# The weights of every second column block of an MLP matrix are split by two transfers and a ScalarE negation

## The chip, the cores and the metric

One NeuronCore of a Trainium2 chip runs the kernel. The metric is the device time of one launch in microseconds (us). A core has TensorE (PE, matrix products; PEld is its loading of weights), VectorE (DVE), ScalarE (ACT), GpSimd (POOL), and SyncE (SP), which issues transfers. Data moves from device memory (HBM) into the on-chip memory SBUF over 16 DMA engines; TensorE writes its sums into PSUM.

## The reference

A hybrid transformer block on 256 latent tokens and 256 context tokens, width 2048, depth 1. The part that the change touches is the MLP at its end:

```python
def sq_relu_mlp(h, w_in, w_out):
    return jnp.square(jax.nn.relu(h @ w_in)) @ w_out

h2 = modulate(rmsnorm(x, norm2_g[i]), sh2, sc2)
x = x + gt2 * sq_relu_mlp(h2, w_mlp_in[i], w_mlp_out[i])
return rmsnorm(x, final_norm_g)
```

`w_mlp_in` is 2048 x 8192, `w_mlp_out` 8192 x 2048. Before it stand a bidirectional gated linear attention, a Fourier branch, their gates and an output projection, and a modulation by products of a vector with a 2048 x 12288 matrix.

## The kernel before

**Precision by splitting.** The inputs are float32. TensorE is fed with a rounded 4-byte type (fp32r). To keep the precision, each operand is held as a high and a low part: `split` lets ScalarE write `hi`, the value rounded to fp32r, and VectorE `lo = value - hi`. A product is then three matmuls (`mm3`): high by high, high by low, low by high. `wide` does the same with fewer instructions: the two parts of the activations lie side by side, 512 columns, and are multiplied with the high part of the weight in one matmul; the low part of the weight is multiplied with the high part of the activations, 256 columns.

**Units.** All weights after the first input projection are laid out in HBM as a list of blocks of 128 x 2048 floats (1 MiB), the tensor `ws`, in the order in which they are used (`stream`). A unit is one such block: 16 weight tiles of 128 x 128, which give 128 output columns. At the end of the list stands the MLP, in four groups g = 0 to 3 of 2048 hidden columns: 16 units `mi` of the first matrix, then 16 units `mo` of the second. The unit `("mi", j)` holds hidden columns 128 j to 128 j + 127. Between them 16 blocks `mod` of the modulation matrix are strewn over the first 76 units or so; VectorE multiplies these in place and sums them (`mod_unit`), and TensorE does not use them.

**Loading and splitting.** `load_to(i)` issues the loads up to block i. Each gets a tile `raw` out of a pool of six (8 KiB in each partition, 1 MiB in all). SP issues them, in order, and its queue waits until a tile is free. `conv_to(i)` splits the units up to i: for each half (`hf`) of a unit it takes two tiles `w` (4 KiB in each partition) out of a pool of eight, and `split` fills them. So eight `w` tiles hold two units. The raw tile is free when the second subtraction has been done, a `w` tile when its matmuls have been done. `next_gemm` is called when a unit is about to be multiplied: it asks for splitting up to the next unit that is not `mod`, and so for loading up to four blocks beyond that one.

**Multiplying.** In g = 0 a unit `mi` runs `unit_mm` with `mm3`, 48 matmuls of 258 columns (256 tokens and two more for the shift of the modulation); in g = 1 to 3 and for all `mo`, `gemm` and `wide` run 16 matmuls of 512 and 16 of 256 columns. The result, one of eight PSUM banks, is copied by ScalarE, added and squared by VectorE, and split again into the tile `hid`, which the units `mo` of the group read.

**Order.** The order in which the program is written gives priorities; a scheduling pass places the instructions of each engine after a simulated timeline. Except for the first part and the tail, which are pinned, it may move instructions past each other. On the chip each engine and each queue works through its list in order. The semaphores for tiles, their reuse among them, are set by the framework.

GpSimd does nothing before but set four constants. Nearly every instruction goes through a recording helper (`call`, line 147), so that the profile gives L147 for almost all of them; groups are told apart by engine, operation and tile.

Of the kernel before, what the change touches and what calls it, by code (L numbers as in the profile page):

```python
# [8 lines left out]
F32R = mybir.dt.float32r  # L9
U32 = mybir.dt.uint32  # L10
AF = mybir.ActivationFunctionType
ALU = mybir.AluOpType

P = 128
D = 2048
T = 256
KT = D // P
# [59 lines left out]
def name_of(tok):  # L77
    k = tok.rstrip("0123456789")
    return k, int(tok[len(k):] or 0)


def stream():
    seq = []
    order = iter([j * 16 + i for j in (0, 2, 1, 3) for i in range(16)])
    for tok in ORDER:
        k, a = name_of(tok)
        if k == "m":
            seq.append(("mod", next(order)))
        elif k in ("oa", "ob"):
            seq.append(("go", 2 * a + (k == "ob")))  # L90
        elif k in ("q", "gf", "gg", "u", "fg", "wo"):
            seq.append((k, a))
    units = []
    for g in range(4):
        units += [("mi", g * 16 + i) for i in range(16)]
        units += [("mo", (g, m)) for m in range(KT)]
    n = 0
    for i, u in enumerate(units):
        seq.append(u)
        while n < min(16, (i + 1) * 16 // FF_RATE):  # L100
            seq.append(("mod", next(order)))
            n += 1
    return seq
# [3 lines left out]
def tile_block(ctx: ExitStack, tc: tile.TileContext, xT, cT, consts, consts2, consts3, masks, dftc, crow, wlr, wma0, wma, wkv, ws, outT):  # L107
    nc = tc.nc
    cst = ctx.enter_context(tc.tile_pool(name="cst", bufs=1))
    rawp = ctx.enter_context(tc.tile_pool(name="rawp", bufs=6))  # L110
# [7 lines left out]
    def nm(s):  # L118
        cnt[0] += 1
        return f"{s}_{cnt[0]}"  # L120
# [4 lines left out]
    def gr(shape):  # L125
        return gp.tile(shape, F32R, tag="g", name=nm("r"))

    def wr(shape):
        return wp.tile(shape, F32R, tag="w", name=nm("w"))
# [4 lines left out]
    def f(ap):  # L134
        return ap.bitcast(F32)
# [15 lines left out]
    V, S, TE, SY = Pinned(nc.vector), Pinned(nc.scalar), Pinned(nc.tensor), Pinned(nc.sync)  # L151

    def split(hi, lo, src):
        S.copy(hi, src)
        V.tensor_tensor(lo, src, f(hi), op=ALU.subtract)
# [18 lines left out]
    def raw(shape):  # L174
        return rawp.tile(shape, F32, tag="raw", name=nm("raw"))
# [278 lines left out]
    seq = stream()  # L454
    NSQ = len(seq)
    unit_raw = {}
    loaded = [0]

    def load_to(i):
        while loaded[0] <= min(i, NSQ - 1):  # L460
            n = loaded[0]
            unit_raw[n] = raw([P, D])
            SY.dma_start(unit_raw[n], ws[n])
            loaded[0] += 1

    conved = {}
    cpos = [0]

    def conv_to(i):
        while cpos[0] <= min(i, NSQ - 1):  # L470
            n = cpos[0]
            load_to(n + 4)
            if seq[n][0] != "mod":
                his, los = [], []
                for hf in range(2):
                    a, b = wr([P, 8, P]), wr([P, 8, P])
                    split(a, b, unit_raw[n][:, hf * 1024:(hf + 1) * 1024].rearrange("p (k c) -> p k c", c=P))
                    his.append(a)
                    los.append(b)
                conved[n] = (his, los)  # L480
            cpos[0] += 1
# [3 lines left out]
    def next_gemm(kind):  # L485
        while True:
            n = pos[0]
            pos[0] += 1
            k, arg = seq[n]
            if k == "mod" and arg >= 48:  # L490
                mod_unit(n, arg)
                continue
            assert k == kind
            nx = n + 1
            while nx < NSQ and seq[nx][0] == "mod":
                nx += 1
            conv_to(nx)
            return n

    def mod_unit(n, i):  # L500
        load_to(n + 3)
        w = D // MSPLIT
        for j in range(MSPLIT):
            sl = slice(j * w, (j + 1) * w)
            V.scalar_tensor_tensor(unit_raw[n][:, sl], unit_raw[n][:, sl], 1.0, cb[:, sl], op0=ALU.mult, op1=ALU.mult,
                                   accum_out=modp[:, i, j:j + 1])
# [48 lines left out]
    def split_v(s, hf):  # L555
        for blk in range(2):
            a, b = gr([P, 512]), gr([P, 512])
            split(a, b, acc[("v", s, blk, hf)])
            vsp[(s, blk, hf)] = (a, b)

    load_to(4)

    def log_sig(pt, shape):
# [359 lines left out]
    for tok in ORDER:  # L923
        k, a = name_of(tok)
# [13 lines left out]
    for g in range(4):  # L938
        hid = []
        for i in range(16):  # L940
# [15 lines left out]
            a = gr([P, 2, T])  # L956
# [206 lines left out]
```

## Time and profile before

| what | us |
|---|---|
| median of 3 runs | 1458.74 (1458.67 to 1459.31) |
| span of the profiled execution, first to last instruction | 1457.3 |
| TensorE busy | 1434.0 |
| VectorE busy | 1072.1 |
| ScalarE busy | 717.7 |
| 16 DMA engines, mean share of the span by queue 1 | 64.1% |

The profiled execution has no time of its own beside the span; the difference of the span to the median, 1.4 us, is taken for what lies around the instructions. The page of the profile gives busy times per engine, a strip of 40 slices, and the chain of waits: from the last instruction back to whatever released it, step by step. A wait is put down to the event that came last. Matmul ends are modelled, since matmuls overlap, so TensorE's busy time is an upper reading. "SPq" and "DVEq" are the instruction queues of an engine, which issue transfers and semaphore operations.

The MLP takes about the second half of the span: its first unit starts near 726 us, and its last ends near 1444 us.

### The profile page before, as it was taken

The page shows a single profiled execution, that of the slowest core. Times are in us where ns is not written, and L with a number is a line of the kernel's source. Part 1 is how long each engine was busy: PE and PEld are TensorE (multiplying, and loading weights), DVE is VectorE, ACT ScalarE, POOL GpSimd, SP SyncE. Part 2 cuts the span into 40 slices and gives each one's busy share as a digit, 9 for nine tenths or more (in the row PEclk, how much of TensorE's full clock was granted, in tenths as well). Part 3 has the DMA queues.
Part 4 walks back from the last instruction along what each step waited for, and adds up shares of the span by engine and source line. Part 5 has one row for each costly group of instructions (what it writes and reads, how often), then busy time and mean ns, then how long its engine had stood idle before and what let it go on. Part 6 is the DMA issues. An engine that isn't in the chain of part 4 may idle for free.

```text
span 1457.3 us, 22947 instructions
## 1 busy us (share of the span) xinstructions
PE 1434.0 (98%) x9352; PEld 1263.9 (87%) x9352; DVE 1072.1 (74%) x1604; ACT 717.7 (49%) x1091; POOL 0.2 (0%) x4
## 2 busy tenths in 40 slices
PE   6999999999999999999999999999999999999997
PEld 3676789999999999999999988888888888888886
DVE  4666688797989889889876776776766666666666
ACT  6333276665645444455644555444334443344553
POOL 0000000000000000000000000000000000000000
PEclk9999999999999999999999999999999999999998
DMA  9967736355578988888866565666665655554531
GB/s 366 341 260 299 271 141 221 139 195 195 202 264 315 352 330 342 327 325 312 323 242 220 204 257 205 227 235 226 233 228 207 253 180 197 179 197 179 196 123 58
DMA packets 52677, 348.54 MB, mean 239 GB/s; under 512 B 5850, under 2 KB 6106, under 8 KB 13020
## 3 DMA queue, kind: packets, MB, share of 16 engines
q1 hardware_dynamic: 52572, 347.08, 64.1%
q8 instruction: 73, 1.20, 0.3%
q14 instruction: 32, 0.26, 0.1%
HBM read 344.96 MB, written 2.10 MB: 238 GB/s over the span
## 4 chain that ended last, share of the span: by engine, by line
PE 98%; DVE 1%; DMA 0%; ACT 0%; SPq 0%; issue 0%; DVEq 0%
PE ps L147 97%; DVE g L147 1%; PE ps L998 1%; DMA g<-in_xT 0%; SPq L147 0%; ACT g L147 0%; ACT r L147 0%; DVEq L1158 0%; DVE AB L147 0%; DVEq L147 0%
## 5 line engine op out<-in xcount | busy, mean ns | idle before, releaser
L147 PE MATMUL ps<-r,w 128*128 128x512 f32 (+2 forms) x7872 | 1213.1, 315 | 0.0
L147 PEld LDWEIGHTS ps<-r,w 128*128 128x128 f32 x7872 | 1101.4, 188 | 108.4 <-issue 2.0
L147 ACT CAST w<-raw 128x1024 fp32r<-128x1024 f32 (+1 forms) x456 | 470.4, 1036 | 584.5 <-PE ps L147 484.1
L147 DVE TENSOR_TENSOR w<-raw,w 128x1024 fp32r<-128x1024 f32 (+1 forms) x456 | 547.8, 1204 | 255.8 <-ACT w L147 253.1
L147 DVE TENSOR_TENSOR g<-ps,g 128x256 f32<-128x256 f32 (+1 forms) x280 | 140.5, 511 | 56.4 <-PE ps L147 55.0
L147 DVE SCALAR_TENSOR_TENSOR raw<-raw,raw 128x2048 f32<-128x2048 f32 x64 | 146.2, 2284 | 3.3 <-DMA raw<-in_ws 3.3
L147 PE MATMUL ps<-w,r 128*128 128x512 f32 x480 | 118.6, 399 | 1.8 <-ACT r L147 1.8
L147 PEld LDWEIGHTS ps<-w,r 128*128 128x128 f32 x480 | 87.7, 188 | 31.3 <-issue 5.4
L147 DVE TENSOR_TENSOR r<-g,r 128x256 fp32r<-128x256 f32 (+2 forms) x184 | 86.8, 482 | 9.7 <-ACT r L147 8.7
L147 ACT CAST r<-g 128x256 fp32r<-128x256 f32 (+2 forms) x184 | 80.8, 454 | 19.7 <-DVE g L147 13.3
L147 ACT COPY g<-ps 128x256 f32<-128x256 f32 (+3 forms) x153 | 60.2, 402 | 51.3 <-PE ps L147 49.4
L147 ACT ACTIVATE g<-g 128x512 f32<-128x512 f32 (+2 forms) x127 | 64.9, 524 | 23.2 <-DVE g L147 18.2
L147 DVE TENSOR_TENSOR g<-g,g 128x256 f32<-128x256 f32 (+2 forms) x99 | 46.0, 489 | 2.2 <-ACT g L147 1.7
L147 ACT ACTIVATE g<-g,AB 128x256 f32<-128x256 f32 x32 | 17.1, 592 | 45.9 <-DVE AB L147 45.9
L147 PE MATMUL ps<-r,r 128*128 128x256 f32 (+2 forms) x282 | 39.0, 286 | 0.0
L147 PEld LDWEIGHTS ps<-r,r 128*128 128x128 f32 (+1 forms) x282 | 36.3, 188 | 1.3 <-DVE r L147 0.2
L147 DVE SCALAR_TENSOR_TENSOR g<-ps,modc,g 128x256 f32<-128x256 f32 (+1 forms) x56 | 25.1, 453 | 13.4 <-PE ps L147 8.8
L147 PE MATMUL ps<-raw,g 128*32 128x512 f32 (+1 forms) x288 | 34.5, 551 | 0.0
L147 PE MATMUL ps<-g,ones 128*32 128x256 f32 (+1 forms) x78 | 14.0, 534 | 10.9 <-ACT g L147 10.9
L147 PEld LDWEIGHTS ps<-raw,g 128*32 128x32 f32 x288 | 8.4, 109 | 15.3 <-issue 13.1
L147 DVE SCALAR_TENSOR_TENSOR g<-g 128x256 f32<-128x256 f32 x48 | 20.4, 425 | 1.4
L147 PEld LDWEIGHTS ps<-g,ones 128*32 128x32 f32 (+1 forms) x78 | 5.7, 146 | 18.0 <-ACT g L147 17.3
(65 smaller groups left out, 254.8 us busy)
## 6 DMA issues: line engine op xcount, KB each, us to landing
raw<-in_ws SPq DMA_DIRECT2D x276, 1024.0 KB, 4.9
raw<-in_wma SPq DMA_DIRECT2D x32, 1024.0 KB, 8.0
raw<-in_wkv SPq DMA_DIRECT2D x16, 784.0 KB, 8.1
g<-in_xT SPq DMA_DIRECT2D x16, 256.0 KB, 6.7
g<-in_cT SPq DMA_DIRECT2D x8, 256.0 KB, 5.7
out<-g SPq DMA_DIRECT2D x8, 256.0 KB, 2.1
raw<-in_crow SPq DMA_DIRECT2D x1, 1024.0 KB, 5.7
g<-in_dftc SPq DMA_DIRECT2D x3, 256.0 KB, 6.8
```

The source lines that it names most:

```text
L147: r = fn(*a, **k)
L998: tc.keep_in_program_order(nc.tensor.matmul(*a, **k))
```

## The change

Units `mi` with an odd number (32 of 64) are no longer split by `split`. Two tiles of the raw pool, typed fp32r, take their parts. A casting transfer issued by GpSimd fills `a` with the high part straight from HBM. ScalarE writes `-a` into `b`, in two halves. For each half another transfer issued by GpSimd reads the same weights again and adds them to `b`, which then holds weight minus high part, the low part. The matmuls read `a` and `b` in place, so both raw tiles are held until the unit's matmuls have been done, and the unit takes no `w` tiles. `conv_to` has nothing to do for it. Even `mi` units, all `mo` units and the `mod` blocks go on as before; the numbers of units and of matmuls stay.

```diff
+    def by_dma(n):
+        return seq[n][0] == "mi" and seq[n][1] % 2 == 1
+
     loaded = [0]
 
     def load_to(i):
         while loaded[0] <= min(i, NSQ - 1):
             n = loaded[0]
-            unit_raw[n] = raw([P, D])
-            SY.dma_start(unit_raw[n], ws[n])
             loaded[0] += 1
+            if not by_dma(n):
+                unit_raw[n] = raw([P, D])
+                SY.dma_start(unit_raw[n], ws[n])
+                continue
+            a, b = (rawp.tile([P, KT, P], F32R, tag="raw", name=nm("raw")) for _ in range(2))
+            w = ws[n].rearrange("p (k c) -> p k c", c=P)
+            nc.gpsimd.dma_start(a, w)
+            for hf in range(2):
+                sl = slice(8 * hf, 8 * hf + 8)
+                S.mul(b[:, sl, :], f(a)[:, sl, :], -1.0)
+                nc.gpsimd.dma_start(b[:, sl, :], w[:, sl, :], accum_op=ALU.add)
+            unit_raw[n] = ([a[:, 0:8, :], a[:, 8:16, :]], [b[:, 0:8, :], b[:, 8:16, :]])
...
-            if seq[n][0] != "mod":
+            if by_dma(n):
+                conved[n] = unit_raw[n]
+            elif seq[n][0] != "mod":
```

## The prediction

> **What bounds the kernel now.** I read the page first (busy shares, slices, chain of waits), then the chain in order of time, then windows over the MLP, because the change touches nothing else.
>
> ```profile
> PE 1434.0 (98%) x9352; PEld 1263.9 (87%) x9352; DVE 1072.1 (74%) x1604; ACT 717.7 (49%) x1091; POOL 0.2 (0%) x4
> PE   6999999999999999999999999999999999999997
> PEclk9999999999999999999999999999999999999998
> PE 98%; DVE 1%; DMA 0%; ACT 0%; SPq 0%; issue 0%; DVEq 0%
> ```
>
> The chain of waits is TensorE for 98% of the span. Its three long pieces, and what follows them (start, duration, engine, tile, line):
>
> ```profile
> 28.21 314.81 PE ps L147 x2016
> 343.05 1091.67 PE ps L147 x7108
> 1434.72 9.71 PE ps L998 x82
> 1444.45 0.36 DVE g L147
> ```
>
> 314.81 + 1091.67 + 9.71 = 1416.19 us, and from 28.21 to 1444.43 there are 1416.22 us: between its first long run and the tail TensorE never waits for anything that ends up on the path. So an edit that leaves every matmul in place can only win what lies before 28 us or after 1444 us, and this one touches neither. The question is whether it can lose.
>
> The windows show the last projection (640 to 720) and the four phases of the first MLP matrix, one for each column group g = 0 to 3. I placed their borders by the tile shapes: 258-column matmuls mark g = 0, and 16 units of each kind follow one another. Columns: window, length, busy time of PE, PEld, DVE, ACT, POOL with counts, granted clock, share of the 16 DMA engines, GB/s.
>
> ```profile
> 640.00:720.00 80.00, 80.00 (x679) 80.00 (x679) 74.57 (x108) 46.91 (x82) 0.00 (x0) 1.00 0.92 350
> 710.00:720.00 10.00, 10.00 (x87) 10.00 (x86) 8.10 (x19) 6.61 (x20) 0.00 (x0) 1.00 1.00 365
> 726.00:818.00 92.00, 92.00 (x766) 91.91 (x765) 66.20 (x93) 45.92 (x69) 0.00 (x0) 1.00 0.62 228
> 908.00:998.00 90.00, 90.00 (x514) 78.51 (x514) 62.10 (x84) 42.56 (x64) 0.00 (x0) 1.00 0.61 223
> 1088.00:1178.00 90.00, 90.00 (x515) 78.54 (x514) 59.96 (x85) 42.29 (x63) 0.00 (x0) 1.00 0.60 222
> 1268.00:1358.00 90.00, 90.00 (x515) 78.50 (x514) 56.14 (x79) 42.45 (x63) 0.00 (x0) 1.00 0.53 187
> ```
>
> TensorE is busy in all of each window at granted clock 1.00. VectorE has a third of its time free, ScalarE half, the DMA engines 38 to 47%. What the change saves on VectorE is time that nobody waits for.
>
> **What is removed.** Of the 64 units of the first MLP matrix the 32 odd ones lose two casts on ScalarE and two subtractions on VectorE each (rows of the whole span, by form):
>
> ```profile
> L147 DVE TENSOR_TENSOR w<-raw,w 128x1024 fp32r<-128x1024 f32 x440 | 537.2, 1222 | 255.0 <-ACT w L147 252.4 <-PE ps L147 0.4
> L147 ACT CAST w<-raw 128x1024 fp32r<-128x1024 f32 x440 | 461.4, 1051 | 576.0 <-PE ps L147 478.8 <-issue 92.8 <-DMA raw<-in_wkv 4.0
> L147 ACT ACTIVATE g<-g 128x512 f32<-128x512 f32 x68 | 41.0, 627 | 12.2 <-DVE g L147 7.5 <-PE ps L147 2.2 <-DMA g<-in_cT 2.0
> L147 ACT ACTIVATE g<-g 128x256 f32<-128x256 f32 x53 | 22.1, 417 | 2.9 <-DVE g L147 2.6
> ```
>
> VectorE: 32 x 2 x 1.222 = 78 us less, on the path 0. ScalarE: 64 casts of 1.051 us go, 64 negations of 128x1024 come. No row shows one; 256 to 512 columns cost 0.417 and 0.627, that is 0.210 for each 256, so 1024 columns are 0.627 + 2 x 0.210 = 1.05 us (an estimate; between 0.63 and 2 x 0.63). ScalarE is unchanged. SP loses 32 issues, Pool gets 96. SP is better off: its next plain load need not wait behind an odd unit for a slot.
>
> **What is added: DMA time.** An odd unit now reads its matrix twice, and the accumulating transfers also read the negated tile in SBUF. A plain 1 MiB load takes 1.049 MB / 365 GB/s = 2.87 us of all 16 engines (window 710 to 720, share 1.00). Issues (KB each, median us to landing):
>
> ```profile
> raw<-in_ws SPq DMA_DIRECT2D x276, 1024.0 KB, 4.9
> raw<-in_wma SPq DMA_DIRECT2D x32, 1024.0 KB, 8.0
> g<-in_dftc SPq DMA_DIRECT2D x3, 256.0 KB, 6.8
> ```
>
> No row shows a casting or an accumulating transfer. The cast cannot cost less than the plain load, 2.87 us; I take that, since it reads and writes the same bytes. Two accumulations of 512 KB: at least 2.87 us; four times that, 11.5 us, if read, read, convert and write each take a pass of their own. I take 5.74 us, nearest to the plain row, because each result byte needs two bytes read. An odd unit is then 3 x 2.87 = 8.61 us of the core's 16 engines, the only ones the profile counts (bounds 5.74 and 14.35).
>
> The Trainium skill bears on this: "Collectives: The Full Stack", in its explanation of why ReduceScatter is half of AllGather, says that the adder in the DMA path costs nothing itself, but that an add needs two source reads on the same ring and so runs at half the copy rate. By that rule the two accumulations are 5.74 us, by a reading in which the add is free 2.87 us; no run here shows it yet.
>
> How much of it must land in time? The unit pitch stands in the DMA queue's own timeline of the last such phase, with the subtraction that lets one load go:
>
> ```profile
> 1284.18 1.23 DVE L147 TENSOR_TENSOR w<-raw,w 128x1024 fp32r<-128x1024 f32 x1 [1.08 <-ACT w L147]
> 1285.43 0.33 SPq L147 DMA_DIRECT2D raw<-in_ws  x1
> 1291.05 0.33 SPq L147 DMA_DIRECT2D raw<-in_ws  x1
> 1296.67 0.33 SPq L147 DMA_DIRECT2D raw<-in_ws  x1
> 1302.29 0.33 SPq L147 DMA_DIRECT2D raw<-in_ws  x1
> ```
>
> The subtraction ends at 1285.41 and the load is issued at 1285.43: loads go out when a raw slot is freed, one each 5.62 us, which is the unit's time on TensorE. I use 5.62 for all four phases (the window of g = 0 holds 766 matmuls, 48 a unit, in 92 us: 5.8 us a unit, a little more room). Six raw slots hold six even units, but an odd one now takes two. So when a phase begins (unit 0 on TensorE), units 0 to 3 fill the slots, and by the start of unit 15 six even and six odd units more must land, with the modulation vectors' blocks between them, 15 x 5.62 = 84.3 us later. Such blocks are the 2048-column operations in the windows of g = 0, 1 and 2; g = 3 has none:
>
> ```profile
> L147 DVE SCALAR_TENSOR_TENSOR raw<-raw,raw 128x2048 f32<-128x2048 f32 x4 | 9.1, 2284 | 0.0
> L147 DVE SCALAR_TENSOR_TENSOR raw<-raw,raw 128x2048 f32<-128x2048 f32 x3 | 6.9, 2284 | 0.0
> L147 DVE SCALAR_TENSOR_TENSOR raw<-raw,raw 128x2048 f32<-128x2048 f32 x2 | 4.6, 2284 | 0.0
> ```
>
> Demand: 6 x 2.87 + 6 x 8.61 = 68.9 us, plus 4, 3, 2, 0 blocks of 2.87: 80.4, 77.5, 74.6, 68.9 of 84.3 us, a share of 0.95, 0.92, 0.88, 0.82. The window 640 to 720 ran at 0.92 with TensorE busy throughout. It fits, with 4 us to spare in g = 0. With the lower bound (5.74 an odd unit) it is 63 us at most.
>
> **What is added: a chain, and waits.** The odd unit's path is: slot a, casting transfer, negation into slot b, accumulation, matmul. When do the slots come free? The eight w tiles hold two even units, and ScalarE's casts wait for TensorE to release them:
>
> ```profile
> ACT w L147 <- PE ps L147: 484.1, 329, 6.1
> ```
>
> So even unit n+3 is split when unit n-1 has left TensorE, done 2.5 us (a cast and a subtraction) after unit n starts; that frees b for odd unit n+4, which starts 4 x 5.62 = 22.5 us after n. That leaves 20.0 us. Slot a is free earlier, when unit n-2 has left TensorE, 5 x 5.62 = 28.1 us before use, so the cast has 8 us before b is there. Handing out slots in stream order is my reading of the pool, not a row. From b on: two negations, 2.1 us, then two accumulations. At least 2.1 + 4.9 = 7.0 us (the MLP's landing time for as many bytes); at most 2.1 + 4 x 6.8 = 29.3 us, if each 512 KB costs two transfers of the 256 KB row, end to end. I take twice the 8.0 us that 1 MiB took when the DMA queue was full early in the kernel: 2.1 + 16 = 18.1 us, within 20.0 but not by much.
>
> The Trainium skill, "DMA: Bandwidth & Descriptors", the anatomy of a Pool-issued transfer, gives 2.0 us plus bytes over 436 GB/s, which by estimate is 3.2 us for 512 KB and a chain of about 8.5 us; no row here shows a transfer issued by Pool.
>
> Waits: a negation on ScalarE waits for the casting transfer; behind it stand the even units' casts and the copies out of PSUM, for which VectorE and then TensorE wait. Even units are split three units ahead and PSUM has eight banks, so a hold of a few us is covered; without that cover it would cost its length. Each accumulation on Pool's queue waits for its negation, and behind it only the next odd unit's cast, whose lead is 8 us longer.
>
> **Sum.** 0 on the path from all parts. The trace's span is 1457.3 us, the median 1458.74, so 1.4 us lie around it: 1457.3 + 1.4 = 1458.7, and with a little for closing one more queue at the end, **1459.0 us**.
>
> **The rivals.**
>
> *Slower, the DMA engines become the bound in the phases of the first matrix.* It decides from an odd unit of (84.3 - 17.2 - 11.5) / 6 = 9.3 us in g = 0 and (84.3 - 17.2) / 6 = 11.2 us in g = 3. At the upper bound, 14.35 us, demand is 103.3 us plus blocks: 30.5 + 27.6 + 24.7 + 19.0 = 102 us over, 1561 us. If cast and accumulation each cost twice the plain bytes (11.5 us an odd unit), 13.3 + 10.4 + 7.5 + 1.8 = 33 us over, 1492 us. For it: shares of 0.82 to 0.95 leave little room, and both new transfer kinds are without a row. Against: it needs more than my price. Chance 0.27.
>
> *Slower, the chain comes late.* If it takes d us more than 20.0, four units take d longer, so d/4 a unit, 4d a phase of 16 units and 16d in all: d = 1 gives 1475 us, the upper bound 29.3 us (d = 9.3) 1608 us. For it: 18.1 us is close, and g = 0 begins just after the stretch at share 1.00, where its first odd unit's transfers fall. Against: the lower bound is 7.0 us. Chance 0.25.
>
> *The negation undoes all of the unit (the cast copies bits and the low part comes out as zero).* All transfers and matmuls stay, so the time is the forecast's, and it is counted there.
>
> *Faster by over 0.2%.* TensorE would have to run the same matmuls quicker; it has no idle time between 28 and 1444 us and the clock is at 1.00. 1455 us or less: chance 0.03.
>
> **How the numbers follow.** Forecast 0.45, DMA bound 0.27, late chain 0.25, faster 0.03. 0.2% (2.9 us) is about what a measurement of this kernel tells from no change. Slower gathers 0.27 + 0.25 = 0.52; most of it is spread thin over 1465 to 1610, so the likeliest single case is no change. The likeliest case's own range is 1457 to 1462. The range to hold 8 in 10 runs from 1456 up to where about half of the DMA-bound case is taken in, between 1492 and 1561: 1530.
>
> **What would show it.** Right: TensorE still fully busy in the four windows, DMA share there near 0.9 to 1.0, VectorE down by some 20 us in each, Pool's transfers landing before 20 us. Wrong: TensorE idle in these windows, released by a DMA into raw (late chain if the share stays below about 0.9, DMA bound if it is near 1.0), or by ScalarE, if held negations stop the PSUM copies. What would make it wrong first is the price of an accumulating transfer.

## The result and the profile after

The changed kernel takes 1504.08 us (median of 4 runs, 1499.49 to 1508.66) against 1458.83 us for the kernel before on the same chip: a ratio of 1.031, 95% interval 1.029 to 1.033. It is 45 us slower. The profiled span is 1501.3 us against 1457.3 us, 44.0 us more.

The page of the kernel after: busy times, slices, DMA queues, chain of waits and issues of transfers.

```profile
PE 1450.8 (97%) x9352; PEld 1274.5 (85%) x9352; DVE 996.4 (66%) x1540; ACT 713.3 (48%) x1091; POOL 73.4 (5%) x100
PE   6999999999999999999989999898999999999997
...
q0 software_dynamic: 13824, 67.12, 18.7%
...
PE 77%; DMA 13%; issue 4%; ACT 3%; DVE 2%; POOL 1%; SPq 0%; POOLq 0%; DVEq 0%; ACTq 0%
...
raw<-in_ws POOLq DMA_DIRECT2D x32, 1024.0 KB, 8.6
raw<-in_ws POOLq DMA_DIRECT2D x64, 512.0 KB, 8.0
```

TensorE runs the same 9352 matmuls and is 16.8 us busier; the other 27.2 of the 44.0 us are idle time. Its chain share fell from 98% to 77%, and 13% went to transfers. Three of the 40 slices now hold an 8: these are in the first MLP matrix. Queue 0 is new and belongs to GpSimd's transfers. New among the waits of TensorE, against the kernel before, are these (engine, tile, line and releaser: us in total, times, longest) and 3.6 us for VectorE's split:

```profile
PE ps L147 <- DMA raw<-in_ws: 19.0, 9, 3.5
PE ps L147 <- ACT w L147: 4.7, 3, 1.7
```

Windows over the four phases of that matrix, g = 0 to 3, kernel after (window, length, busy time of PE, PEld, DVE, ACT, POOL with counts, granted clock, DMA share, GB/s):

```profile
720.00:840.00 120.00, 110.53 (x854) 108.34 (x854) 54.60 (x101) 49.47 (x90) 16.20 (x21) 0.96 0.86 249
900.00:1040.00 140.00, 128.29 (x693) 110.27 (x692) 63.35 (x95) 57.69 (x88) 17.67 (x23) 0.95 0.83 246
1090.00:1240.00 150.00, 143.67 (x802) 123.59 (x801) 74.75 (x111) 61.01 (x82) 18.21 (x24) 0.99 0.86 261
1280.00:1400.00 120.00, 120.00 (x686) 104.77 (x685) 58.80 (x91) 53.63 (x74) 17.72 (x23) 1.00 0.87 250
```

TensorE waits 9.5, 11.7 and 6.3 us in g = 0, 1 and 2, and in g = 3 not at all, at the highest DMA share of the four. Late in g = 3 the DMA engines are full, and TensorE is busy throughout:

```profile
1360.00:1380.00 20.00, 20.00 (x116) 17.43 (x115) 9.55 (x16) 9.02 (x15) 3.83 (x5) 1.00 1.01 256
```

So a full set of DMA engines is a poor explanation. g = 3 differs in having no `mod` blocks and, as shown below, in having one more slot.

How a stall comes about is seen in two timelines of g = 1, kernel after (start, duration, engine, line, operation, tiles, count, and in brackets the idle time before and its releaser). First GpSimd's queue; line 473 issues the cast, line 477 the two accumulations:

```profile
918.27 0.55 POOL L473 DMA_DIRECT2D raw<-in_ws  x1 [12.46 <-ACT w L147]
924.75 1.79 POOL L477 DMA_DIRECT2D raw<-in_ws  x2 [5.92 <-ACT raw L147]
934.26 0.56 POOL L473 DMA_DIRECT2D raw<-in_ws  x1 [7.72 <-PE ps L147]
941.90 1.79 POOL L477 DMA_DIRECT2D raw<-in_ws  x2 [7.09 <-ACT raw L147]
945.74 0.55 POOL L473 DMA_DIRECT2D raw<-in_ws  x1 [2.04 <-PE ps L147]
957.68 1.80 POOL L477 DMA_DIRECT2D raw<-in_ws  x2 [11.39 <-DVE w L147]
959.21 0.83 POOL L473 DMA_DIRECT2D raw<-in_ws  x1
974.67 1.80 POOL L477 DMA_DIRECT2D raw<-in_ws  x2 [14.62 <-ACT raw L147]
```

And TensorE; groups with `raw` read a transferred unit (an odd one), groups with `w` a split one:

```profile
939.65 5.78 PE L147 MATMUL ps<-r,raw 128*128 128x512 f32 x32
945.27 5.78 PE L147 MATMUL ps<-r,w 128*128 128x512 f32 x32
950.89 5.78 PE L147 MATMUL ps<-r,raw 128*128 128x512 f32 x32
956.51 5.78 PE L147 MATMUL ps<-r,w 128*128 128x512 f32 x32
962.13 0.40 PE L147 MATMUL ps<-r,raw 128*128 128x512 f32 x1
964.21 0.51 PE L147 MATMUL ps<-r,w 128*128 128x512 f32 x1 [1.68 <-ACT w L147]
967.00 7.20 PE L147 MATMUL ps<-r,raw 128*128 128x256 f32 x31 [2.29 <-DMA raw<-in_ws]
974.04 5.58 PE L147 MATMUL ps<-r,w 128*128 128x256 f32 x31
979.46 0.40 PE L147 MATMUL ps<-r,raw 128*128 128x512 f32 x1
983.33 2.08 PE L147 MATMUL ps<-r,raw 128*128 128x256 f32 x9 [3.47 <-DMA raw<-in_ws]
```

The cast at 945.74 waited for TensorE ("<-PE ps"): the odd unit that TensorE had begun at 939.65 ended near 945.4, and its two slots came free. This cast is for the odd unit that starts at 962.13, two odd units later. Its lead is 962.13 - 945.74 = 16.4 us; the cast before had 950.89 - 934.26 = 16.6 us. The unit's first matmul finds the high part at 962.13, but the low part's accumulations were only issued at 957.68, and TensorE waits for them until 967.00. (Between the two it waited 1.68 us for the split of the next even unit.) The next odd unit, cast at 959.21, is late as well: TensorE waits 3.47 us for it.

What the 16 DMA engines did meanwhile, from 944 to 975 us in 40 equal slices (busy share in tenths):

```profile
DMA  8997999999999600002579989988999999999504
```

They are full to about 954 us, idle from 955 to 958, and full again to 973. They stand idle shortly before TensorE does: GpSimd's accumulations at 957.68 had waited 11.39 us. Then the held transfers go out almost together and lengthen each other. The phase's mean of 0.83 hides both.

Why two odd units and not three? `cb`, the vector that the `mod` blocks are multiplied with, is a tile of the same pool of six. It is written in the first part and read by every `mod` block, the last of them in g = 2. Through g = 0, 1 and 2 five slots are left, and the `mod` blocks' loads pass through those. Two odd units in flight take four. My prediction counted six. In g = 3, where `cb` is gone, the sixth odd unit has its cast, its accumulations (GpSimd) and its matmuls (TensorE) here:

```profile
1345.33 0.87 POOL L473 DMA_DIRECT2D raw<-in_ws  x1
1359.79 1.83 POOL L477 DMA_DIRECT2D raw<-in_ws  x2 [3.62 <-ACT raw L147]
1372.02 5.78 PE L147 MATMUL ps<-r,raw 128*128 128x512 f32 x32
```

From the cast to the accumulations it took 14.5 us, no less than the 11.9 us of the late unit in g = 1. But the lead is 1372.02 - 1345.33 = 26.7 us, and TensorE doesn't wait.

### The profile page after: what moved, and what is told of

It reads as the page before. It is cut to its first block, busy times and chain, and to the rows that moved or that the text cites. A ratio compares the mean times of both kernels' runs of the same rounds, so it can differ in the third digit from the quotient of the medians.

```text
span 1501.3 us, 23029 instructions
## 1 busy us (share of the span) xinstructions
PE 1450.8 (97%) x9352; PEld 1274.5 (85%) x9352; DVE 996.4 (66%) x1540; ACT 713.3 (48%) x1091; POOL 73.4 (5%) x100
## 3 DMA queue, kind: packets, MB, share of 16 engines
q0 software_dynamic: 13824, 67.12, 18.7%
## 4 chain that ended last, share of the span: by engine, by line
PE 77%; DMA 13%; issue 4%; ACT 3%; DVE 2%; POOL 1%; SPq 0%; POOLq 0%; DVEq 0%; ACTq 0%
PE ps L147 77%; DMA raw<-in_ws 12%; ACT raw L147 1%; DVE g L147 1%; POOL raw L477 1%; PE ps L1014 1%; DVE w L147 1%; ACT g L147 0%; ACT w L147 0%; DMA g<-in_xT 0%; ACT r L147 0%; DVE raw L147 0%; DMA g<-in_cT 0%; SPq L147 0%; DVE r L147 0%
## 5 line engine op out<-in xcount | busy, mean ns | idle before, releaser
L147 PE MATMUL ps<-r,w 128*128 128x512 f32 (+2 forms) x6720 | 1042.7, 315 | 8.4 <-ACT w L147 4.7
L147 PEld LDWEIGHTS ps<-r,w 128*128 128x128 f32 x6720 | 943.0, 189 | 101.3 <-ACT w L147 5.9
L147 DVE TENSOR_TENSOR w<-raw,w 128x1024 fp32r<-128x1024 f32 (+1 forms) x392 | 467.4, 1199 | 212.6 <-ACT w L147 208.1
L147 ACT CAST w<-raw 128x1024 fp32r<-128x1024 f32 (+1 forms) x392 | 401.2, 1033 | 433.6 <-PE ps L147 341.6
L147 PE MATMUL ps<-r,raw 128*128 128x258 f32 (+2 forms) x1152 | 199.8, 331 | 19.1 <-DMA raw<-in_ws 19.0
L147 PEld LDWEIGHTS ps<-r,raw 128*128 128x128 f32 x1152 | 174.1, 198 | 40.4 <-DMA raw<-in_ws 22.9
L147 ACT ACTIVATE raw<-raw 128x1024 fp32r<-128x1024 f32 x64 | 64.2, 1052 | 98.4 <-DMA raw<-in_ws 83.6
L473 POOL DMA_DIRECT2D raw<-in_ws x32 | 21.6, 675 | 1063.2 <-DMA raw<-in_ws 705.7
L477 POOL DMA_DIRECT2D raw<-in_ws x64 | 55.3, 869 | 247.7 <-ACT raw L147 233.0
```

Source lines behind the costliest of these rows:

```text
L147: r = fn(*a, **k)
L473: nc.gpsimd.dma_start(a, w)
L477: nc.gpsimd.dma_start(b[:, sl, :], w[:, sl, :], accum_op=ALU.add)
```

## The experiments

Theory A: the raw slots are too few, so the transfers are issued too late. Theory B: the DMA engines are full. Theory C: the order of GpSimd's queue holds the next cast back behind the accumulations. Each run stands beside runs of the kernel before on the same chip (1458.8 to 1459.2 us); 95% intervals of the ratio in brackets. "MLP time" is from the first 258-column matmul to the end of the span: 732.4 us before, 776.2 after.

**e4, without the accumulating transfers.**

```diff
                 S.mul(b[:, sl, :], f(a)[:, sl, :], -1.0)
-                nc.gpsimd.dma_start(b[:, sl, :], w[:, sl, :], accum_op=ALU.add)
```

> The 64 accumulating transfers are left out, so the low part of the odd units is just minus the high part; cast and negation stay. An odd unit then costs 2.8 us of the DMA engines in place of 8.7, and its chain is some 9 us shorter; slots stay. All of A, B and C expect most of the loss to go, 1458 to 1470 us; if the time stays above 1485 us, the loss is in the casting transfer or in the slots alone, whatever the chain's length.

Measured: 1459.77 us, 1.0003 [0.9993, 1.0012], MLP time 733.0. Casts, negations and two slots a unit remain, and cost nothing. The loss comes with the accumulating transfers, by their DMA time or by how long they keep slots; this run doesn't tell which.

**e1, a slot given back**, by keeping `cb` in a bfloat16 tile of its own, paid for with two small tiles.

```diff
-NSLOT = 54
+NSLOT = 52
...
-    cb = raw([P, D])
-    SY.dma_start(cb, crow)
+    cb0 = raw([P, D])
+    SY.dma_start(cb0, crow)
+    cb = cst.tile([P, D], mybir.dt.bfloat16, name="cb")
```

> The vector cb, which every modulation block is multiplied with, moves out of the raw pool into a tile of its own (in bfloat16, so that it fits; two of 54 small tiles are given up for it), so the units of g = 0, 1 and 2 have six raw slots instead of five; the modulation sums are a little less exact. Theory A (slots: odd units wait for a pair of raw slots, of which cb holds one): most of the 45 us goes, 1460 to 1475 us, and the casting transfers of g = 1 are issued earlier before their use. Theory B (DMA engines are full because of the modulation blocks' bytes): unchanged, 1495 to 1510 us. Theory C (GpSimd's queue is in order and a cast stands behind the accumulations of the unit before): 1490 us or more.

Measured: 1507.61 us, 1.0327 [1.031, 1.0344]. A's number was missed, but the run mixes two things: the MLP begins at 755.9 instead of 725.0 us, because the parts ahead of it became slower, and its own time fell from 776.2 to 751.5. Which of the two edits delayed the start stays open.

**e2, the slot held to the end** by a late read of `cb`.

```diff
+    hold = cst.tile([P, 1], F32, name="hold")
+    V.tensor_copy(hold, cb[:, 0:1])
```

> One read of cb is added at the end, so cb holds its raw slot through g = 3 too; nothing else changes. Theory A: g = 3, which did not stall, now stalls like the others: 9 to 16 us more, 1513 to 1520 us, with idle TensorE in its phase of the first matrix. Theories B and C: no more than 2 us more, since bytes and order stay.

Measured: 1503.05 us, 1.0306 [1.0289, 1.0324]. It says nothing: the read had nothing to wait for, and the scheduling pass moved it to 212 us, so the slot was not held longer.

**e9, the same with a read that can't move**: it also uses `ssum`, which exists only when the MLP's sums do.

```diff
+    hold = cst.tile([P, 1], F32, name="hold")
+    V.tensor_tensor(hold, cb[:, 0:1], ssum[:, 0:1], op=ALU.mult)
     units = [conved.pop(next_gemm("mo")) for _ in range(2)]
```

> The read that was to hold cb was placed at 212 us, where its operands were ready, and so held nothing. Here it also reads the last sum of squares, which is ready only at the end, so that g = 3 has five raw slots and still no modulation block. Theory A (slots): g = 3 loses about what g = 0 loses with five slots and the blocks elsewhere (15 us, first to last 258-column matmul 108.3 us against 92.6 before): 1514 to 1522 us. Theory B (DMA engines full): within 2 us of the change, since no byte is added.

Measured: 1524.42 us, 1.0449 [1.0431, 1.0467], 20.3 us above the change. The window of g = 3, which had no stall in the kernel after, in e9, and the one behind it, in which the phase ends:

```profile
1280.00:1400.00 120.00, 115.33 (x645) 99.56 (x644) 54.30 (x83) 47.40 (x64) 16.45 (x22) 0.99 0.73 210
1400.00:1460.00 60.00, 53.70 (x298) 46.30 (x297) 32.49 (x46) 27.89 (x40) 1.71 (x2) 0.94 0.68 242
```

TensorE now waits 4.7 and 6.3 us there, at a DMA share of 0.73 instead of 0.87 in the first. No byte was added; one slot was taken. That is what A says, and B can't say it. The total is a little above A's range: beside the 11.0 us stand a lower clock and 3.4 us more of waits in g = 0 to 2, for which I have no reason.

**e3, the `mod` blocks out of these phases**, all between `mo` units of g = 0 and 1.

```diff
-        while n < min(16, (i + 1) * 16 // FF_RATE):
+        while u[0] == "mo" and n < min(16, (16 * (u[1][0]) + u[1][1] + 1) // 2):
```

> The 16 modulation blocks of the MLP all go between the units of the second matrix in g = 0 and 1, so that no such block is loaded within a phase of the first matrix; cb keeps its slot until the end of g = 1. Theory A: g = 2 has six slots and stalls no more, g = 0 and 1 keep five slots but no block passes through them: 1475 to 1495 us. Theory B: all stalls go, 1459 to 1465 us. Theory C: 1490 us or more.

Measured: 1494.98 us, 1.0245 [1.0228, 1.0263], MLP time 766.3. Windows of g = 1 and 2 in e3:

```profile
900.00:1040.00 140.00, 127.68 (x702) 109.11 (x701) 63.99 (x98) 59.08 (x89) 18.18 (x24) 0.98 0.80 240
1090.00:1240.00 150.00, 149.76 (x854) 130.48 (x854) 77.14 (x116) 63.89 (x86) 18.34 (x24) 1.00 0.87 265
```

`cb` is now free after g = 1, and g = 2 stops stalling with a DMA share that is no lower than before the edit (0.87 against 0.86). g = 1, where `cb` still sits, goes on stalling at 0.80, though no block is multiplied there before the last odd unit now. The total alone lies in C's range as well as in A's.

**e5, `cb` out of the pool** from g = 0 on: ScalarE copies it into a tile that is dead by then. **e6** is its control, the same copy in the kernel before.

```diff
+    cbs = [cb]
+    def move_cb():
+        c2 = big.tile([P, D], F32, tag="big", name="cb2")
+        S.copy(c2, cb)
+        cbs[0] = c2
...
-        "df": lambda _: dft3(),
+        "df": lambda _: (dft3(), move_cb()),
```

> The first try to free cb's raw slot also changed what runs ahead of the MLP (its first unit began at 755.9 us, not 725.0), so its total says nothing; from that unit to the end it took 751.5 us, against 776.2 with the change and 732.4 before. Here cb is copied once, with the Fourier branch, into the tile kq, which is dead by then, and the pool of small tiles keeps its 54. Theory A (slots): the MLP takes about 751 us and the whole 1476 to 1484 us, if the part ahead of it stays. Theory B (the DMA engines are full): the MLP stays at 770 us or more, 1495 us or more.

> Control: the same copy of cb in the kernel before, without the change. All theories: within 4 us of the kernel before, 1456 to 1463 us, since TensorE binds there; if it is slower, as much is to be taken off the run with cb out.

Measured: e6 1467.15 us, 1.0057 [1.0042, 1.0072], so the copy itself costs 8.3 us, more than expected, of which 6 us are a later start of the MLP (730.9). e5 1485.21 us, 1.0175 [1.0158, 1.0192], MLP time 752.4: of the 43.8 us that the change adds to the MLP, 23.8 are gone. The MLP time is what A expected; the total is 1 us above A's range, which left out the price of the copy.

**e7, both**: `cb` out of the pool and the blocks out of the phases.

> cb out of the raw pool and the modulation blocks between the units of the second matrix. Theory A: six slots, none of them taken by a block in a phase of the first matrix, as g = 3 has them, which ran without a stall: 1459 to 1466 us. Theory B: as with the blocks moved alone, 1490 to 1497 us. Theory C (order of GpSimd's queue): 1480 us or more.

Measured: 1469.73 us, 1.0078 [1.0056, 1.0101], 2.6 us above the control e6, MLP time 739.1. The window of g = 0, first in e5:

```profile
720.00:840.00 120.00, 116.29 (x923) 114.53 (x922) 63.63 (x116) 57.96 (x105) 16.34 (x21) 0.99 0.95 286
```

and in e7:

```profile
720.00:840.00 120.00, 120.00 (x956) 117.94 (x955) 61.25 (x113) 61.38 (x108) 16.51 (x22) 1.00 0.95 276
```

In the kernel after, TensorE waited 9.5 us here at a share of 0.86; in e7 it never waits at 0.95, with every cast and accumulation still made. TensorE's waits in the windows of g = 0, 1 and 2 (us, length less busy time) side by side:

| run | `cb` | blocks | g = 0 | g = 1 | g = 2 |
|---|---|---|---|---|---|
| the change | in the pool | in the phases | 9.5 | 11.7 | 6.3 |
| e3 | in the pool, free from g = 2 | out | 11.1 | 12.3 | 0.2 |
| e5 | out | in the phases | 3.7 | 5.2 | 4.2 |
| e7 | out | out | 0.0 | 2.6 | 1.0 |

With `cb` in the pool, moving the blocks away wins nothing in g = 0 and 1; with `cb` out, it wins another 2.5 to 3.7 us in each phase. So B falls as the bound of these phases, and more than half of the loss hangs on the one slot. The blocks take both a slot and DMA time, and no run separates these for the 13.3 us of MLP time between e5 and e7. Against the control, e7's MLP time is still 4.7 us longer (734.4 in e6).

**e8, the low part unread**: odd units' matmuls read the high part twice, all transfers stay.

```diff
-            unit_raw[n] = ([a[:, 0:8, :], a[:, 8:16, :]], [b[:, 0:8, :], b[:, 8:16, :]])
+            unit_raw[n] = ([a[:, 0:8, :], a[:, 8:16, :]], [a[:, 0:8, :], a[:, 8:16, :]])
```

> All transfers, negations and queues stay, but the matmuls of the odd units read the high part in place of the low one, so TensorE waits for the casting transfer alone and b is freed when its accumulations have landed (the low part is left out of the product). If only the last link is late (accumulations land after their use): 1459 to 1470 us. If the DMA engines are full, the even units and the casts come late all the same: 1485 us or more.

Measured: 1493.69 us, 1.024 [1.0221, 1.0258]; 10.4 us of 45 come back. In the timeline of g = 1 it was the accumulation that TensorE waited for at 967.00; but with that wait gone most of the loss remains. The time is the one expected for full DMA engines; that the casts, and the loads that queue for the same slots, are late for want of slots would give it as well, and this run doesn't tell which. In g = 3, which had not stalled, TensorE now waits 4.9 us for splits of even units, though `b` is freed earlier; why stays open.

**e10, the next cast ahead of the low part** of the odd unit before it, on GpSimd's queue and in the handing out of slots.

```diff
             nc.gpsimd.dma_start(a, w)
+            low_to(n - 1)
+            later.append((n, a, w))
```

(`low_to` takes slot `b` and issues negations and accumulations; `conv_to` calls it for the unit's own number.)

> In the order of the program the casting transfer of the next odd unit comes ahead of the negation and the accumulations of the one before, so that on GpSimd's queue it is not held by a negation. Slots and bytes stay. Theory C (the queue's order holds the casts): 1475 us or less. Theory A: a cast that goes first takes the slot that the older unit's b needs, so nothing is won: 1495 us or more. Theory B: unchanged.

Measured: 1515.53 us, 1.0389 [1.0373, 1.0406]: 11 us slower than the change. C's forecast fails, and A's holds. My reading is that a cast that is issued earlier keeps its slot longer; no run shows that alone. The order isn't free of effect, though: in the timeline of g = 1 the cast at 959.21 went out right behind the accumulations, 2.5 us after TensorE had left the unit begun at 950.89 (950.89 + 5.78 = 956.67). e10 changes the handing out of slots too, so it doesn't show what such holds cost.

**e11, `b` in two `w` tiles** in place of a raw slot.

```diff
-            a, b = (rawp.tile([P, KT, P], F32R, tag="raw", name=nm("raw")) for _ in range(2))
+            a = rawp.tile([P, KT, P], F32R, tag="raw", name=nm("raw"))
+            b = [wr([P, 8, P]) for _ in range(2)]
```

> The low part of an odd unit goes into two tiles of the w pool, which odd units leave free, in place of a raw tile, so an odd unit holds one raw slot. cb keeps its slot, the modulation blocks stay where they are; the bytes stay. Theory A: raw slots suffice; even units are split later, because fewer w tiles are free: 1459 to 1470 us. Theory B: 1495 us or more.

Measured: 1593.83 us, 1.0927 [1.0901, 1.0953], a miss. The waits of e11 (engine, tile, line and releaser: us in total, times, longest):

```profile
POOL w L478 <- ACT w L147: 260.0, 33, 12.8
...
PE ps L147 <- ACT w L147: 95.0, 20, 12.1
```

TensorE now waits for ScalarE's writing of `w`. The eight `w` tiles held two even units of two high and two low halves each; the odd units take two of them for as long as a transfer needs, and the splits have no room. The shortage moved to another pool. The run doesn't count against A, but doesn't support it either.

**e12, every third unit** (21 instead of 32).

```diff
-        return seq[n][0] == "mi" and seq[n][1] % 2 == 1
+        return seq[n][0] == "mi" and seq[n][1] % 3 == 1
```

> Every third unit of the first MLP matrix (21 or 22 of 64) is split by transfers, with cb in its slot and the modulation blocks in place. A budget of slot time from the trace with the change: an odd unit held its two slots 27 and 22 us (49 slot-us), an even one needs at least 4.8 us for its load and 2.4 us for its split (7.2), a block 4.8 + 2.3, one in 4.75 units. With every second unit, 11.24 us and five slots: 56.2 there, 49 + 7.2 + 3.0 = 59 wanted. With every third, 16.9 us: 84 there, 49 + 14.4 + 4.5 = 68 wanted. Theory A: it fits, 1459 to 1466 us. If the length of the chain itself were the bound, whatever the slots: two thirds of the loss stay, 1485 to 1492 us.

Measured: 1478.99 us, 1.0134 [1.0117, 1.0151], between the two expectations, which both missed. A had counted the even units' loads and the blocks at 4.8 us, as long as a lone one takes. Rows of e12's chain in order of time (start, duration, what):

```profile
974.41 13.61 DMA raw<-in_ws
990.40 15.47 DMA raw<-in_ws
```

In a stalled stretch one transfer takes 13.6 or 15.5 us, against medians of 6.5 (cast) and 10.0 (accumulation) over the run, so each slot is held longer than counted. How much of this remainder is lengthened transfers and how much is the order in which slots are handed out stays open; no run separates them.

No version beats the kernel before: the nearest that does all the work is e7, at 1.0078.

## Why the prediction was right or wrong

**The bound: right.** TensorE sets the end, and the change could only lose.

**What is removed: right.** The by-form rows of the kernel after for the subtraction and the negation:

```profile
L147 DVE TENSOR_TENSOR w<-raw,w 128x1024 fp32r<-128x1024 f32 x376 | 456.8, 1221 | 211.7 <-ACT w L147 207.4 <-PE ps L147 3.6
...
L147 ACT ACTIVATE raw<-raw 128x1024 fp32r<-128x1024 f32 x64 | 64.2, 1052 | 98.4 <-DMA raw<-in_ws 83.6 <-DVE w L147 8.6 <-issue 6.3
```

64 subtractions are gone and VectorE is busy 1072.1 - 996.4 = 75.7 us less (78 predicted), which bought nothing. A negation takes 1.052 us (1.05 predicted).

**The DMA time of an odd unit: right.** Queue 0 took 18.7% of 1501.3 us for 32 units, 8.77 us each; I had taken 8.61 between 5.74 and 14.35. By the trace's packet records a cast costs 2.80 and the two accumulations 5.89 us of 16 engines. The Trainium skill's rule in "Collectives: The Full Stack" (the explanation of why ReduceScatter is half of AllGather: an add costs its two source reads) gave 5.74, and the trace agrees with 5.89. So the DMA-bound rival, at 0.27, whose threshold was 9.3 us in g = 0, didn't come about, and e7 shows a share of 0.95 carried without a wait. This price was named as what would make the prediction wrong first; it held.

**The lead: wrong, and this is the step that failed.** "Six raw slots hold six even units", and "Slot a is free earlier, when unit n-2 has left TensorE, 5 x 5.62 = 28.1 us before use". The trace has 16.4 and 16.6 us in g = 1, because `cb` keeps one slot through g = 2 and the `mod` blocks use the others too. The code showed it: `cb = raw([P, D])` is a tile of the pool, and its last reader is the last block. I counted the blocks' bytes in the demand and left their slots, and the vector's, out of the supply. In g = 3, where six slots are there, the lead is 26.7 us, near the 28.1, and the forecast of no wait holds. e9 (one slot less in g = 3: stall), e3 and e5 (the slot of `cb` back: stalls go or shrink) and e7 show it.

**The chain: right in size where I priced it, short where I didn't.** From the first negation (956.33, in ScalarE's timeline) to the landing of the last accumulation (969.49) the late unit took 13.2 us; I had 18.1. But the cast ahead of it, for which I allowed 8 us, has a median of 8.6; the late unit's took 9.8, and others grew more in the stalled stretches. The chain of the kernel after in order of time, whose steps at 959.21 and 976.15 begin with the cast issued then:

```profile
959.21 14.00 DMA raw<-in_ws
...
976.15 13.07 DMA raw<-in_ws
```

From issue of the cast to the last landing the late unit took 969.49 - 945.74 = 23.8 us: within 28.1, but 7.4 us more than 16.4. The rival "the chain comes late" so named the right wait, TensorE released by a DMA into raw at a share below 0.9, with the wrong cause: the chain was too long for the lead that was left, not for the lead I had counted. It was its start that I had wrong.

**The hold on ScalarE: right in the main.** Negations waited 98.4 us in all, but TensorE waited for ScalarE's casts into `w` only three times, 4.7 us in total, against 19.0 us for transfers.

**A term that was missing: the clock.** Windows of the kernel after over the two late units of g = 1, and over one behind them:

```profile
967.00:974.00 7.00, 7.00 (x31) 6.10 (x32) 1.07 (x3) 1.09 (x2) 0.00 (x0) 0.76 0.91 335
983.40:990.40 7.00, 7.00 (x32) 6.07 (x33) 0.09 (x1) 1.07 (x2) 0.00 (x0) 0.76 0.91 335
1001.80:1007.10 5.30, 5.30 (x33) 4.67 (x32) 0.03 (x1) 1.11 (x2) 0.00 (x0) 1.00 1.05 272
```

The same number of matmuls takes 7.0 us at a granted clock of 0.76 and 5.3 at 1.00. By the clock records the MLP ran at half clock six times, 27.3 us in all, in 25.1 of which TensorE was busy; at half speed that costs about 12.5. With 27.2 us of idle time that is about 40 of the 44 us: more than a quarter of the loss is the clock, and some 4 us are not accounted for.

**The range** held by luck: it reached to 1530 to take in part of the DMA-bound rival, which didn't come about. The forecast, no change, was off by 45 us, and the likeliest case's own range, 1457 to 1462, failed.

## What to carry to other kernels

Work that is moved from an engine to transfers pays in buffer time: multiply the slots that each unit holds by how long it holds them, with transfer times taken beside other traffic, and compare with the slots that are really free. Read the share of the DMA engines in short slices: a mean over a phase can hide that they are idle and then full. Look for long-lived tiles in the same pool before counting it, and for every other user that passes through it. And where TensorE has been busy without a break, add to a stall the time at a lower clock behind it.

## What the hardware showed that I had not expected

The clock falls after short waits. In g = 1 TensorE waited 1.68 and 2.29 us with half a microsecond of work between, and the granted clock was 0.5 for 3.4 us from 967.58 on. The Trainium skill, "TensorE: Matmul & The Clock Gate", Part 1, ties the half clock to at least one idle window of about 3.4 us; the 3.4 us of half clock agree with its window, but here no single wait before it reached 3.4 us.

Transfers in flight together lengthen each other, and the mean share doesn't show it. A cast of 1 MiB landed in 5.0 us where the DMA engines were half busy (918.27; share 0.51 from 918 to 924), and in 14.00 us in the stall (959.21; share 1.00 from 959.2 to 973.2), while the window of the phase shows 0.83. When the accumulations are left out (e4), the median of the casts over the run is 5.4 instead of 8.6 us.
